# A transformer-style block in fp32 products on one core: two of the four weight sums move to GpSimd, and spills and reloads to SyncE's queue

## The chip, the core and the metric

The kernel runs on one core of a Trainium2 chip. The metric is device time in microseconds (us); lower is better. Engines are named as the profile does: PE (TensorE; PEld is its weight load), DVE (VectorE), ACT (ScalarE), POOL (GpSimd), SP (SyncE, which here issues DMAs only).

## What is computed

One layer of a streaming encoder with 256 rows, 2048 columns, in fp32. Cut to its products:

```python
h = rms_norm(x, norm_mix)
proj = h @ w_in                       # 2048 x 11264: two mixers and two gates
y_a = hgrn2_mixer(...)                # gated recurrence
y_b = chunked_relpos_attention(...)
merged = sigmoid(gate_a) * (y_a @ w_proj_a) + sigmoid(gate_b) * (y_b @ w_proj_b)
x = x + merged @ w_out                # 2048 x 2048
h = rms_norm(x, norm_ffn)
g, u = split(h @ w_ffn_in)            # 2048 x 11264
x = x + (silu(g) * u) @ w_ffn_out     # 5632 x 2048
```

## The kernel before

**Products.** Every weight is read once, in blocks of 512 rows by 512 columns; a block arrives as two tiles `raw` of 128x1024 (512 KB each; eight buffers). An fp32 product is made of three products of rounded parts: ACT casts a weight tile to `whi`, DVE subtracts to get the rest, `wlo`, and PE runs three matmuls (high by high, high by low, low by high) for each tile of activations and columns. `whi` and `wlo` have four buffers each. In a plain product (`product`, lines 156 to 173) each `raw` costs one cast (L147) and one subtraction (L148).

**Pairs of products.** `product_pair` (L206 and on) works on two column blocks at once and saves one eighth of PE's work in chosen steps: in one use of 512 rows, the first two of four k-tiles go through seven products instead of eight (a Strassen scheme in Winograd's form), the other two go plainly. The seven products need sums of weights. `weight_forms` (L185 to L203) makes them on DVE from four quarter tiles b11, b21, b12, b22 of 128x512: `ta` = (b12 - b11, b22 - b12) and then `tb` = (ta0 - b22, b21 + tb0), all four through the helper at L194; each pair is split into `whi` and `wlo` as a raw tile is (`halves`, `split`, L177 and L178). `ta` and `tb` share two buffers (tag `t6`), so the next `ta` waits until the last one is split. There are 46 uses: gate blocks (2 pairs of products, 4 uses each), w_out (1 pair, 4 uses), w_ffn_in (5 pairs, 4 uses each) and w_ffn_out (2 pairs, 7 uses each of 11 steps). A pair with four uses is called a stage below.

**Order of work.** A scheduler in the language's tile layer sets each engine's order from priorities; `high_priority` in `product_pair` lets the weight preparation run ahead of the matmuls it is for, as far as buffers allow. Each engine then works through its own list in order, and waits on semaphores.

**Sums of activations.** `act_forms` (L318) makes the activation side of the seven products (`sf`, then a split into `fm`, `fx`, `fq`, `sform`); its inputs in `transpose_split` (L305) come from PE transposes in PSUM. In the first feed-forward product the sums of seven steps (`sform`) are spilled to DRAM (`kept`, L315) and read back before the last product (`sf`, L907). The residual `x` is spilled at L843 and read back at L912; `x_forms` (L753) reads quarter rows of `x_t` again at L759. In the kernel before, these five kinds of DMA are issued by POOL; all weights are issued by SP (L130), in a list of its own that also waits in order.

The lines that the change touches are L194 to L198 in `weight_forms`, and L315, L759, L843, L907 and L912.

Of the kernel before, what the change touches and what calls it, by code (L numbers as in the profile page):

```python
# [10 lines left out]
F32 = mybir.dt.float32  # L11
# [3 lines left out]
ALU = mybir.AluOpType  # L15
# [30 lines left out]
def block_kernel(ctx: ExitStack, tc: tile.TileContext, x, x_t, w_in, w_pa, w_pb, w_out, w_fi, w_fo,  # L46
                 params, b_gate, bias, masks, out):
    nc = tc.nc
# [14 lines left out]
    def nm(s):  # L63
        uid[0] += 1
        return f"{s}_{uid[0]}"

    def t4(shape, s, dt=F32):
        return big.tile(shape, dt, tag="t4", name=nm(s))
# [29 lines left out]
    def add(out, a, b):  # L98
        nc.vector.tensor_tensor(out=out, in0=a, in1=b, op=ALU.add)
# [18 lines left out]
    def start(g):  # L118
        running.append(g)
# [60 lines left out]
    def halves(src):  # L180

        n = src.shape[1]
        hi = whi_p.tile([P, 2, 512], F32R, tag="hi", name=nm("whi"))
        lo = wlo_p.tile([P, 2, 512], F32R, tag="lo", name=nm("wlo"))
        split(hi[:, 0:n, :], lo[:, 0:n, :], src)  # L185
        return [(hi[:, k, :], lo[:, k, :]) for k in range(n)]

    def weight_forms(r0, r1):


        ta = t6_p.tile([P, 2, 512], F32, tag="t6", name=nm("ta"))
        tb = t6_p.tile([P, 2, 512], F32, tag="t6", name=nm("tb"))
        b11, b21, b12, b22 = r0[:, 0, :], r0[:, 1, :], r1[:, 0, :], r1[:, 1, :]
        op = lambda out, x, y, o: nc.vector.tensor_tensor(out=out, in0=x, in1=y, op=o)  # L194
        p1, p2 = halves(r0)
        p3, = halves(r1[:, 1:2, :])
        op(ta[:, 0, :], b12, b11, ALU.subtract)
        op(ta[:, 1, :], b22, b12, ALU.subtract)  # L198
        p5, p7 = halves(ta)
        op(tb[:, 0, :], ta[:, 0, :], b22, ALU.subtract)  # L200
        op(tb[:, 1, :], b21, tb[:, 0, :], ALU.add)
        p6, p4 = halves(tb)
        return {1: p1, 2: p2, 3: p3, 4: p4, 5: p5, 6: p6, 7: p7}  # L203
# [72 lines left out]
    def split_tiles(s):  # L276
        return (t4([P, 4, T], s + "h", F32R), t4([P, 4, T], s + "l", F32R))
# [11 lines left out]
    def transpose_split_pair(nat, pair, hi, lo, gain=None, pool=aux):  # L289

        pt = transpose_pair(nat, pair, pool)
        if gain is None:
            sl = slice(2 * pair, 2 * pair + 2)
            nc.scalar.copy(hi[:, sl, :], pt)
            nc.vector.tensor_tensor(out=lo[:, sl, :], in0=pt, in1=hi[:, sl, :].bitcast(F32),
                                    op=ALU.subtract)
            return pt
        for j in range(2):
            k = 2 * pair + j
            nc.scalar.activation(hi[:, k, :], pt[:, j, :], AF.Copy, scale=gain[:, k:k + 1])  # L300
            nc.vector.scalar_tensor_tensor(out=lo[:, k, :], in0=pt[:, j, :],
                                           scalar=gain[:, k:k + 1],
                                           in1=hi[:, k, :].bitcast(F32),
                                           op0=ALU.mult, op1=ALU.subtract)
        return pt  # L305

    def transpose_split(nat, hi, lo, gain=None, wait=2, pool=aux, forms=None, spill=None):
        for _ in range(wait):
            yield 1
        for pair in range(2):  # L310
            pt = transpose_split_pair(nat, pair, hi, lo, gain, pool)
            if forms is not None and pair == 0:
                act_forms(pt, forms, gain)
                if spill is not None:
                    nc.gpsimd.dma_start(out=spill, in_=forms.bitcast(F32))  # L315
            yield 1

    def act_forms(pt, f, gain=None):  # L318

        s = t2([P, 4, P], "sf")  # L320
        a11, a21, a12, a22 = (pt[:, k, m * P:(m + 1) * P] for k in range(2) for m in range(2))

        def op(out, x, k, y, o):
            if gain is None:
                nc.vector.tensor_tensor(out=out, in0=x, in1=y, op=o)
            else:
                nc.vector.scalar_tensor_tensor(out=out, in0=x, scalar=gain[:, k:k + 1], in1=y,
                                               op0=ALU.mult, op1=o)

        if gain is None:  # L330
            nc.scalar.copy(s[:, 2, :], a21)
        else:
            nc.scalar.activation(s[:, 2, :], a21, AF.Copy, scale=gain[:, 0:1])
        op(s[:, 0, :], a22, 1, s[:, 2, :], ALU.add)
        op(s[:, 2, :], a11, 0, s[:, 2, :], ALU.subtract)
        op(s[:, 1, :], a11, 0, s[:, 0, :], ALU.subtract)
        op(s[:, 3, :], a12, 1, s[:, 1, :], ALU.add)
        split(f[:, 0], f[:, 1], s)
# [9 lines left out]
    xs = []  # L348
# [4 lines left out]
    def sumsq_block(src, ss, c):  # L353
        for m in range(2):
            junk = t2([P, 512], "junk")
            nc.scalar.activation(junk, src[:, m, :], AF.Square, accum_out=ss[:, m, c:c + 1])
# [228 lines left out]
    def hgrn_mix(half, b, kk, qT, v, sg, hi, lo):  # L585
# [26 lines left out]
        for i in range(2):  # L612
# [15 lines left out]
            for h in range(4):  # L628
# [3 lines left out]
                                               op0=ALU.mult, op1=ALU.mult)  # L632
            yield 1
        yield from transpose_split(y, hi, lo, gain, wait=2)


# [118 lines left out]
    def x_forms():  # L755

        for c in range(4):
            xt = t4([P, 2, T], "xt2")
            nc.gpsimd.dma_start(out=xt, in_=x_t[c, :, 0:2, :])  # L759
            fq[c] = t4([P, 2, 4, P], "fq", F32R)  # L760
            yield 1
            yield 1
            act_forms(xt, fq[c], par[:, C_NM + 4 * c:C_NM + 4 * c + 4])

    gates, fq = {}, {}
    start(x_forms())
    for nb in range(4):
        bgs, gts = [], []
        for br in range(2):
            c = 4 * br + nb  # L770
# [6 lines left out]
            for m in range(2):  # L777
                nc.vector.scalar_tensor_tensor(out=gt[:, m, :], in0=ps[m], scalar=r1[:, m:m + 1],
                                               in1=bgs[br], op0=ALU.mult, op1=ALU.add)
# [37 lines left out]
    x2T, x2_kept, fx = [], [], {}  # L817
    ss2 = cpool.tile([P, 2, 4], F32, tag="ss2", name="ss2")
    r2 = cpool.tile([P, 2], F32, tag="r2", name="r2")
    def residual_sums(x0, x1):  # L820
        def sums(ub):
            u2, u3 = t2([P, 512], "u2"), t2([P, 512], "u3")
            add(x0[:, 0, :], x0[:, 0, :], ub[1])
            nc.scalar.copy(u2, ub[1])
            add(u2, ub[6], u2)
            add(u3, ub[7], u2)
            add(x1[:, 0, :], x1[:, 0, :], u2)
            add(x0[:, 1, :], x0[:, 1, :], u3)
            add(x1[:, 1, :], x1[:, 1, :], u3)
            for m in range(2):  # L830
                add(x1[:, m, :], ub[5], x1[:, m, :])
        return sums

    def norm_block(nb, ps):
        for m in range(2):
            add(xs[nb][:, m, :], ps[m], xs[nb][:, m, :])
        x2T.append(split_tiles("x2T"))
        fx[nb] = t4([P, 2, 4, P], "fx", F32R)
        start(transpose_split(xs[nb], *x2T[nb], gain=par[:, C_NF + 4 * nb:C_NF + 4 * nb + 4],
                              forms=fx[nb]))  # L840
        sumsq_block(xs[nb], ss2, nb)
        x2_kept.append(dram.tile([P, 2, 512], F32, tag=f"x2_{nb}", name=nm("x2")))
        nc.gpsimd.dma_start(out=x2_kept[nb], in_=xs[nb])  # L843

    for pair in range(2):
        nbs = (2 * pair, 2 * pair + 1)
# [13 lines left out]
    kept = {}  # L860
# [22 lines left out]
    for j in range(NJ):  # L883
# [12 lines left out]
        if j in SEVEN:  # L896
            f = t4([P, 2, 4, P], "sform", F32R)
            spill = kept[j] = dram.tile([P, 2, 4, P], F32, tag=f"kept{j}", name=nm("kept"))
# [5 lines left out]
    forms = {}  # L904
    for j in SEVEN:
        forms[j] = t4([P, 2, 4, P], "sf", F32R)
        nc.gpsimd.dma_start(out=forms[j].bitcast(F32), in_=kept[j])  # L907
    for pair in range(2):
        nbs = (2 * pair, 2 * pair + 1)
        xs = {nb: t4([P, 2, 512], "x2") for nb in nbs}  # L910
        for nb in nbs:
            nc.gpsimd.dma_start(out=xs[nb], in_=x2_kept[nb])  # L912
        x0, x1 = (xs[nb] for nb in nbs)

        pools = (mm, aux) if pair == 0 else (aux, mm)
        cb = product_pair(w_fo, nbs, NJ, act_h, forms, *pools,
                          residual_sums(x0, x1), last=pair == 1)
        for n, nb in enumerate(nbs):
            for m in range(2):
                pieces = 2 if nb == 3 and m == 1 else 1  # L920
                w = 512 // pieces
                for i in range(pieces):
                    sl = slice(i * w, (i + 1) * w)
                    add(xs[nb][:, m, sl], cb[m, n][:, sl], xs[nb][:, m, sl])
                    nc.sync.dma_start(out=out_v[:, m, nb * 512 + i * w:nb * 512 + (i + 1) * w],
                                      in_=xs[nb][:, m, sl])
# [63 lines left out]
```

## Time and profile before

| what | value |
|---|---|
| median of 3 runs | 1428.09 us (1427.48 to 1429.13) |
| the profiled execution, its own time | 1427.22 us |
| its span in the profile | 1425.4 us |
| PE busy | 1417.6 us (99%) |
| DVE busy | 1063.6 us (75%) |
| ACT busy | 774.2 us (54%) |
| POOL busy | 50.1 us (4%) |
| DMA, mean | 202 GB/s |

The span is what the trace covers; the time of the run is 1.8 us longer. Busy shares are averages over the whole span. Whether an engine is on the path is read from what the next engine was waiting for at that moment, and with how much to spare.

### The profile page before, as it was taken

Reading aid. Unit: us, or ns where it says so; the run is one execution under the profiler, and the core shown is the slowest. Engines: PE = TensorE matmul, PEld = TensorE weight load, DVE = VectorE, ACT = ScalarE, POOL = GpSimd, SP = SyncE. Lnnn points to the kernel's source line nnn. Section 1 sums busy time; section 2 is a strip of 40 time slices with the busy share of each in tenths; the row PEclk is TensorE's granted clock in tenths of the full one; section 3 lists DMA queues with packets and bytes.
Section 4 is the critical chain, followed back from the end, with each engine's and each line's share of the span. In section 5 each row is a group of like instructions: output and inputs, shape, how many; then the busy total and the mean of one; then the engine's idle time right before and its main releaser. Section 6 shows DMA issues by size and latency. Waiting matters only on the chain.

```text
span 1425.4 us, 17596 instructions
## 1 busy us (share of the span) xinstructions
PE 1417.6 (99%) x6448; PEld 1174.4 (82%) x6448; DVE 1063.6 (75%) x1361; ACT 774.2 (54%) x1009; POOL 50.1 (4%) x63
## 2 busy tenths in 40 slices
PE   9999999999999999999999999999999999999998
PEld 7888888888888888878888888888788888888887
DVE  6768869564878697689767769687796876777875
ACT  7756565555655454455555546455454554544553
POOL 0100100100000000100000000000000010000000
PEclk9999999999999999999999999999999999999999
DMA  9654354446657556547654657656476578666652
GB/s 360 243 192 161 134 193 156 164 163 195 222 183 240 197 197 210 184 148 239 220 203 168 228 169 240 206 179 228 164 238 206 178 254 303 210 221 221 208 183 84
DMA packets 81848, 288.37 MB, mean 202 GB/s; under 512 B 9185, under 2 KB 9441, under 8 KB 81761
## 3 DMA queue, kind: packets, MB, share of 16 engines
q1 hardware_dynamic: 78272, 274.66, 57.5%
q0 software_dynamic: 3488, 12.58, 2.3%
q8 instruction: 50, 0.82, 0.2%
q14 instruction: 38, 0.30, 0.1%
HBM read 279.34 MB, written 7.86 MB: 201 GB/s over the span
## 4 chain that ended last, share of the span: by engine, by line
PE 98%; DVE 1%; ACT 0%; DMA 0%; issue 0%; SPq 0%; DVEq 0%; ACTq 0%
PE mm L169 18%; PE mm L168 18%; PE mm L170 18%; PE mp L223 13%; PE mp L224 13%; PE mp L222 13%; PE bank L285 2%; PE bank L543 1%; DVE wlo L178 1%; ACT whi L177 0%; PE bank L573 0%; DMA raw<-in_w_in 0%; PE bank L619 0%; PE bank L670 0%; PE bank L698 0%; DVE tb L194 0%
## 5 line engine op out<-in xcount | busy, mean ns | idle before, releaser
L148 DVE TENSOR_TENSOR wlo<-raw,whi 128x1024 fp32r<-128x1024 f32 (+1 forms) x292 | 351.9, 1212 | 175.6 <-ACT whi L147 173.4
L147 ACT CAST whi<-raw 128x1024 fp32r<-128x1024 f32 (+1 forms) x292 | 301.9, 1040 | 292.7 <-PE mm L170 219.8
L178 DVE TENSOR_TENSOR wlo<-raw,whi 128x1024 fp32r<-128x1024 f32 x216 | 235.0, 1110 | 51.9 <-ACT whi L177 50.8
L177 ACT CAST whi<-raw 128x1024 fp32r<-128x1024 f32 x216 | 201.2, 960 | 121.8 <-PE mp L224 59.6
L168 PE MATMUL mm<-whi,xTh 128*128 128x512 f32 x576 | 226.6, 398 | 1.3 <-ACT whi L147 1.3
L169 PE MATMUL mm<-wlo,xTh 128*128 128x512 f32 x576 | 225.2, 391 | 0.0
L170 PE MATMUL mm<-whi,xTl 128*128 128x512 f32 x576 | 225.1, 391 | 0.0
L168 PE MATMUL mm<-whi,x2Th 128*128 128x512 f32 x384 | 150.0, 391 | 0.0
L170 PE MATMUL mm<-whi,x2Tl 128*128 128x512 f32 x384 | 149.5, 389 | 0.0
L169 PE MATMUL mm<-wlo,x2Th 128*128 128x512 f32 x384 | 149.4, 389 | 0.0
L168 PEld LDWEIGHTS mm<-whi,xTh 128*128 128x128 f32 x576 | 108.2, 188 | 23.0 <-ACT whi L147 2.0
L170 PEld LDWEIGHTS mm<-whi,xTl 128*128 128x128 f32 x576 | 108.2, 188 | 22.6
L169 PEld LDWEIGHTS mm<-wlo,xTh 128*128 128x128 f32 x576 | 108.3, 188 | 21.8 <-DVE wlo L148 1.0
L223 PE MATMUL mp<-wlo,hTh 128*128 128x512 f32 x282 | 109.7, 389 | 0.0
L224 PE MATMUL mp<-whi,hTl 128*128 128x512 f32 x282 | 109.6, 389 | 0.0
L222 PE MATMUL mp<-whi,hTh 128*128 128x512 f32 x282 | 99.7, 390 | 0.0
L177 ACT CAST whi<-ta 128x1024 fp32r<-128x1024 f32 x46 | 48.3, 1050 | 89.9 <-PE mp L224 87.4
L178 DVE TENSOR_TENSOR wlo<-ta,whi 128x1024 fp32r<-128x1024 f32 x46 | 56.2, 1223 | 48.3 <-ACT whi L177 48.3
L224 PE MATMUL mp<-whi,x2Tl 128*128 128x512 f32 x220 | 86.2, 392 | 0.0
L223 PE MATMUL mp<-wlo,x2Th 128*128 128x512 f32 x220 | 86.2, 392 | 0.0
L170 PEld LDWEIGHTS mm<-whi,x2Tl 128*128 128x128 f32 x384 | 72.1, 188 | 15.0
L168 PEld LDWEIGHTS mm<-whi,x2Th 128*128 128x128 f32 x384 | 72.1, 188 | 14.8
(256 smaller groups left out, 2260.8 us busy)
## 6 DMA issues: line engine op xcount, KB each, us to landing
raw<-in_w_fi SPq DMA_DIRECT2D x176, 512.0 KB, 4.4
raw<-in_w_in SPq DMA_DIRECT2D x172, 512.0 KB, 4.1
raw<-in_w_fo SPq DMA_DIRECT2D x88, 512.0 KB, 5.3
raw<-in_w_out SPq DMA_DIRECT2D x32, 512.0 KB, 4.3
raw<-in_w_pa SPq DMA_DIRECT2D x16, 512.0 KB, 3.7
raw<-in_w_pb SPq DMA_DIRECT2D x16, 512.0 KB, 4.3
x<-x POOLq DMA_DIRECT2D x8, 512.0 KB, 5.7
kept<-sform POOLq DMA_DIRECT2D x7, 512.0 KB, 4.9
```

The costliest lines, as they stand in the source:

```text
L147: nc.scalar.copy(hi[:, sl, :], src[:, sl, :])
L148: nc.vector.tensor_tensor(out=lo[:, sl, :], in0=src[:, sl, :], in1=hi[:, sl, :].bitcast(F32), op=ALU.subtract)
L168: nc.tensor.matmul(ps[m], lhsT=ah, rhs=wh, start=kc == 0 and k4 == 0, stop=False)
L169: nc.tensor.matmul(ps[m], lhsT=ah, rhs=wl, start=False, stop=False)
L170: nc.tensor.matmul(ps[m], lhsT=al, rhs=wh, start=False, stop=kc == n_chunks - 1 and k4 == 3)
L177: nc.scalar.copy(hi, src)
L178: nc.vector.tensor_tensor(out=lo, in0=src, in1=hi.bitcast(F32), op=ALU.subtract)
L222: nc.tensor.matmul(ps, lhsT=ah, rhs=wh, start=first, stop=False)
L223: nc.tensor.matmul(ps, lhsT=ah, rhs=wl, start=False, stop=False)
L224: nc.tensor.matmul(ps, lhsT=al, rhs=wh, start=False, stop=final)
L285: nc.tensor.transpose(out=pt[:, j, m * P:(m + 1) * P], in_=nat[:, m, c:c + P], identity=ident)
L543: nc.tensor.matmul(pl[:, j, :], lhsT=ek[:, g // 2, (g % 2) * P:(g % 2 + 1) * P], rhs=eq[:, g, :], start=True, stop=True)
```

## The change

Two of the four sums in `weight_forms` (those of `ta`) are issued on GpSimd instead of VectorE, 92 instructions in all. The 26 DMAs that POOL issued (four reads of `x_t`, four spills of `x`, seven spills of `sform`, their seven and four reloads) are issued by SyncE's queue.

```diff
@@ weight_forms
-        op(ta[:, 0, :], b12, b11, ALU.subtract)
-        op(ta[:, 1, :], b22, b12, ALU.subtract)
+        for i, (x, y) in enumerate(((b12, b11), (b22, b12))):
+            nc.gpsimd.tensor_tensor(out=ta[:, i, :], in0=x, in1=y, op=ALU.subtract)
         p5, p7 = halves(ta)
@@ transpose_split
-                    nc.gpsimd.dma_start(out=spill, in_=forms.bitcast(F32))
+                    nc.sync.dma_start(out=spill, in_=forms.bitcast(F32))
@@ x_forms
-            nc.gpsimd.dma_start(out=xt, in_=x_t[c, :, 0:2, :])
+            nc.sync.dma_start(out=xt, in_=x_t[c, :, 0:2, :])
@@ norm_block
-        nc.gpsimd.dma_start(out=x2_kept[nb], in_=xs[nb])
+        nc.sync.dma_start(out=x2_kept[nb], in_=xs[nb])
@@ before the last product
-        nc.gpsimd.dma_start(out=forms[j].bitcast(F32), in_=kept[j])
+        nc.sync.dma_start(out=forms[j].bitcast(F32), in_=kept[j])
...
-            nc.gpsimd.dma_start(out=xs[nb], in_=x2_kept[nb])
+            nc.sync.dma_start(out=xs[nb], in_=x2_kept[nb])
```

The scheduler puts the new lists together. On DVE, in the w_ffn_in stage around 943 us of the profile (the numbers behind names tell buffers apart: ta_7922 is the `ta` of this use, tb_7840 the `tb` of the use before, raw_7833 and raw_7837 weight tiles that go plainly):

```order
 L178 TENSOR_TENSOR wlo_7852<-ta_7839,whi_7851 128x1024
 L178 TENSOR_TENSOR wlo_7858<-tb_7840,whi_7857 128x1024
-L194 TENSOR_TENSOR ta_7922<-raw_7918,raw_7914 128x512
-L194 TENSOR_TENSOR ta_7922<-raw_7918 128x512
 L178 TENSOR_TENSOR wlo_7862<-raw_7833,whi_7861 128x1024
+L194 TENSOR_TENSOR tb_7923<-ta_7922,raw_7918 128x512
 L178 TENSOR_TENSOR wlo_7866<-raw_7837,whi_7865 128x1024
-L194 TENSOR_TENSOR tb_7923<-ta_7922,raw_7918 128x512
 L178 TENSOR_TENSOR wlo_7925<-raw_7914,whi_7924 128x1024
```

The two subtractions leave DVE's list, and the first sum of `tb` moves up by one instruction, ahead of the split of raw_7837.

On SP's list, where the last product begins, around 1197 us of the profile (raw tiles are weights of w_ffn_out, the x tiles the residual's third and fourth block, read back):

```order
 L130 DMA raw_10102<-in_w_fo 128x1024
 L130 DMA raw_10104<-in_w_fo 128x1024
+L912 DMA x_2185_10752<-x_1153_5807 128x1024
+L912 DMA x_2186_10753<-x_1188_5990 128x1024
 L130 DMA raw_10106<-in_w_fo 128x1024
 L130 DMA raw_10108<-in_w_fo 128x1024
```

The two reloads now stand between weight loads, and raw_10106 is issued behind whatever they wait for.

## Rows read from the trace of the kernel before

**Rows 1.** The page, part 1: busy time of each engine, share, instructions.

```profile
PE 1417.6 (99%) x6448; PEld 1174.4 (82%) x6448; DVE 1063.6 (75%) x1361; ACT 774.2 (54%) x1009; POOL 50.1 (4%) x63
```

**Rows 2.** Waits: who waited for whom, us in total, times, longest.

```profile
PEld mp L222 <- ACT whi L177: 3.2, 6, 1.0
PEld mp L223 <- DVE wlo L178: 2.5, 7, 0.5
```

**Rows 3.** Groups by line: busy us, mean ns of one.

```profile
L194 DVE TENSOR_TENSOR ta<-raw,raw 128x512 f32<-128x512 f32 x46 | 32.1, 697 | 15.8 <-DMA raw<-in_w_fi 8.2 <-DMA raw<-in_w_fo 4.3 <-DMA raw<-in_w_in 1.8
L194 DVE TENSOR_TENSOR ta<-raw 128x512 f32<-128x512 f32 x46 | 31.5, 685 | 0.0
```

**Rows 4.** DVE's busy time in one stage of w_ffn_in (stretch, length, busy).

```profile
930.00:971.00 41.00, 35.75 (x42) 1.00 0.55 185
```

**Rows 5.** Line 809 on POOL: duration ns min/median/max.

```profile
L809 POOL TENSOR_TENSOR gate<-gate,gate x8: 1293/1521/2280, 554.9 to 624.5; 128x512 f32<-128x512 f32 x8
```

**Rows 6.** Timeline of POOL, 62 to 65 us: start, us, engine, line, operation.

```profile
62.33 2.01 POOL L559 COPY eq<-qT 128x1024 f32<-128x1024 f32 x1 [23.88 <-DVE qT L473]
64.28 1.07 POOL L521 COPY eq<-b 128x512 f32<-128x512 f32 x1
```

**Rows 7.** Timeline of DVE, the same stretch.

```profile
62.21 1.23 DVE L148 TENSOR_TENSOR wlo<-raw,whi 128x1024 fp32r<-128x1024 f32 x1
63.35 1.52 DVE L564 TENSOR_TENSOR eq<-eq,qT 128x512 f32<-128x512 f32 x1
```

**Rows 8.** Timeline of DVE, 934 to 949 us, a stage of w_ffn_in.

```profile
934.53 1.23 DVE L178 TENSOR_TENSOR wlo<-ta,whi 128x1024 fp32r<-128x1024 f32 x1 [2.29 <-ACT whi L177]
...
937.96 1.23 DVE L178 TENSOR_TENSOR wlo<-tb,whi 128x1024 fp32r<-128x1024 f32 x1 [0.26 <-ACT whi L177]
...
942.64 1.22 DVE L178 TENSOR_TENSOR wlo<-ta,whi 128x1024 fp32r<-128x1024 f32 x1
943.92 1.23 DVE L178 TENSOR_TENSOR wlo<-tb,whi 128x1024 fp32r<-128x1024 f32 x1
945.06 0.69 DVE L194 TENSOR_TENSOR ta<-raw,raw 128x512 f32<-128x512 f32 x1
...
946.26 2.36 DVE L178 TENSOR_TENSOR wlo<-raw,whi 128x1024 fp32r<-128x1024 f32 x2
948.54 0.69 DVE L194 TENSOR_TENSOR tb<-ta,raw 128x512 f32<-128x512 f32 x1
```

**Rows 9.** Timeline of PE: first matmuls on the two tiles of the x2 row above.

```profile
947.56 0.48 PE L223 MATMUL mp<-wlo,x2Th 128*128 128x512 f32 x1
...
950.17 0.39 PE L223 MATMUL mp<-wlo,x2Th 128*128 128x512 f32 x1
```

**Rows 10.** Timeline of DVE, 857 to 862 us, a stage with activation sums in it.

```profile
857.17 1.22 DVE L178 TENSOR_TENSOR wlo<-tb,whi 128x1024 fp32r<-128x1024 f32 x1
...
859.51 1.22 DVE L178 TENSOR_TENSOR wlo<-raw,whi 128x1024 fp32r<-128x1024 f32 x1
...
861.85 2.96 DVE L178 TENSOR_TENSOR wlo<-raw,whi 128x1024 fp32r<-128x1024 f32 x3
```

**Rows 11.** Timeline of PE: first matmul on the first tile of the x3 row above.

```profile
863.88 0.39 PE L223 MATMUL mp<-wlo,x2Th 128*128 128x512 f32 x1
```

**Rows 12.** Timeline of DVE in the last product, at a use behind a use.

```profile
1211.51 1.22 DVE L178 TENSOR_TENSOR wlo<-ta,whi 128x1024 fp32r<-128x1024 f32 x1 [1.40 <-ACT whi L177]
...
1214.23 1.23 DVE L178 TENSOR_TENSOR wlo<-tb,whi 128x1024 fp32r<-128x1024 f32 x1 [0.17 <-ACT whi L177]
```

**Rows 13.** Timeline of PE: first matmul on the last tile of rows 12.

```profile
1216.57 0.39 PE L223 MATMUL mp<-wlo,sf 128*128 128x512 f32 x1
```

**Rows 14.** Timeline of POOL: a spill, and the last reload.

```profile
861.74 0.53 POOL L315 DMA_DIRECT2D kept<-sform  x1 [44.39 <-DVE sform L178]
...
1202.80 0.54 POOL L912 DMA_DIRECT2D x<-x  x1 [11.05 <-PE bank L285]
```

**Rows 15.** Timeline of SP: the weight loads that stand around these two.

```profile
860.75 2.67 SPq L130 DMA_DIRECT2D raw<-in_w_fi  x2
...
1206.66 0.33 SPq L130 DMA_DIRECT2D raw<-in_w_fo  x1
```

## The prediction

> **What bounds the kernel now.** I read the shares first: PE is busy in 99% of the span, DVE in 75%, POOL in 4% [rows 1]. The reader is to see from this that relief on DVE can buy little by itself: PE never lacks work for long. The waits come next: in the pairs of products, PE's weight loads waited for a cast 6 times, 3.2 us in all, and for DVE's `wlo` 7 times, 2.5 us [rows 2]. These 5.7 us are about all that a faster preparation of weights could give back there. The third view is a stage by itself: in a stage of w_ffn_in DVE is busy 35.75 of 41 us [rows 4], far more than its average. The fourth is the timeline inside such a stage, with DVE's and PE's rows side by side. There DVE works without a gap from 942.64 to 949 us [rows 8], and its two splits of plain weights end at about 947.5 and at 948.62 (946.26 + 2.36). PE takes the first up at 947.56 and the second at 950.17 [rows 9]; which matmul uses which tile I took from the numbers in the two lists. So the spare time is nearly nothing for the one and 1.55 us for the other. The stage runs at PE's speed, but with DVE close behind: whatever delays DVE there by more than a microsecond reaches PE.
>
> **The change, part by part.**
>
> *What leaves DVE.* 92 subtractions of 0.69 us, 63.6 us busy [rows 3]. They follow each other closer than that: two take the time from 945.06 to 946.26, so 0.60 us each [rows 8], and 1.2 us for each of 46 uses.
>
> *What POOL takes on.* POOL already does the same operation on the same shape at L809: 1293 ns at best, 2280 ns at worst [rows 5]. I take 1.29 us as the run by itself. 92 of them are 119 us on an engine that is busy for 50 us [rows 1], so POOL as such does not become a bound.
>
> *What the two engines do to each other.* This is the term that decides. At 62.21 DVE starts a split with two operands in SBUF; its next instruction is issued at 63.35 and shows 1.52 us for 512 columns, where 0.69 is usual [rows 3, 7]. POOL's copy is issued at 62.33 and shows 2.01 us; the next, at 64.28, shows 1.07 us for half the columns [rows 6]. Laid side by side: POOL waits until the split ends at 63.4 and runs to 64.3; DVE's next, issued in between, waits until 64.3 and runs to 64.9; only then POOL's next one runs. They take turns, whole instructions at a time, and the one that has waited goes first. The spread at L809 fits, since 2.28 is 1.29 and most of a split of 1.22. So while both have work, each POOL subtraction stops DVE for 1.29 us and saves it 0.60. A use costs DVE between -1.2 us (POOL hits idle time, or a DVE instruction that reads one operand from PSUM) and 2 x (1.29 - 0.60) = +1.4 us. In gapless stretches I take the upper value, in others I follow the rows.
>
> [...]
>
> *An ordinary stage, worked through.* The next `ta` may start once the last one is split (two shared buffers). First use: the split of `ta` ends at 935.76 (934.53 + 1.23). POOL runs to 937.1 and to 938.4. DVE's split of `tb` could start at 937.96 [rows 8], so it is 0.44 late, and the chain behind it is packed. Next use: the split of `ta` ends at 943.86, DVE's split of `tb` starts at 943.92 and is ahead of POOL. It hands over after 1.14 us (945.06). Then in turn: POOL to 946.35, DVE's first plain split to 947.49, POOL to 948.78, DVE's sum `tb` to 949.38 (it now stands ahead of the second plain split), and the second plain split ends 1.22 later, at 950.60. Before it ended at 948.62. PE wants it at 950.17: 0.43 late. With the 0.44 carried in, PE loses 0.9 us in this stage. Three stages of w_ffn_in (930 us is the middle one) and two of the gates have this shape: 5 x 0.9 = 4.4 us.
>
> *The stages with activation sums.* Where the step before has its sums spilled, `act_forms` falls into the stage and DVE has no gap at all. After the split of `tb` at 857.17 POOL takes over at 858.31 (to 859.60), DVE's plain split, before at 859.51, hands over at 860.74, POOL runs to 862.03. Then `tb` and the split of `sform`, 0.60 each, to 863.23, and the next plain split ends at 864.45. Before it ended at 863.07 (861.85 + 1.22) [rows 10]; PE wants it at 863.88 [rows 11]: 0.57 late, with the same 0.44 carried in 1.0. There are three such stages (w_out, and two of w_ffn_in): 3.0 us.
>
> *The last product.* Its margins are wider. The split of `ta` ends at 1212.73, POOL runs to 1214.1 and 1215.4, so the split of `tb` starts 1.15 late, not at 1214.23, and ends at 1216.6 [rows 12]; PE wants it at 1216.57 [rows 13]. That is some 0.1 us where a use follows a use directly, 8 times: 0.8 us. The six others lie beside steps without sums, and I cost them at nothing; that work hides up to 2.6 us each.
>
> *The DMAs.* 26 issues go from POOL's list to SP's. SP waits in order, so a reload that waits for a buffer would hold up weights. But the scheduler put each behind a weight load that was issued late enough already: the spill that POOL issued at 861.74 comes between two loads issued from 860.75 on and ending at 863.42, and the last reload, which waited until 1202.80, stands ahead of a load that was issued only at 1206.66 [rows 14, 15]. I cost them at 0. If that cover went, a load would be later by the difference, and DVE's and ACT's lists would wait for the weights behind it. The four reads of `x_t` come later than before, on the way to sums that are needed only in the first gate stage: 0.
>
> *Sum.* 4.4 + 3.0 + 0.8 + 0 = +8.2 us, on the profiled execution's own 1427.22 us: **1435.4 us**. That execution lies 0.9 us under the median of the runs. Neither end of the unknown is far: without any collision the gain is at most the 5.7 us of rows 2; with every margin used up by the full 1.4 us in all 46 uses the loss would be 64 us, but DVE has 5.25 us to spare in a stage of 41 [rows 4], against 4 x 1.4 = 5.6. So a stage can hardly lose more than 2 us, 16 in all.
>
> **The rivals.** About 0.2% (2.9 us) is what a measurement of this kernel can tell from no change.
>
> 1. *The collisions stay hidden.* If POOL's pairs mostly fall into DVE's idle time, or a first delay of PE buys spare time for all that follows, the losses stay under 2.9 us: 1427 to 1430. For it speaks that PE's lateness is not added up use by use, against it the 0.1 us to spare at 947.56. Chance 0.20.
>
> 2. *DVE's relief reaches PE: faster.* The waits of rows 2 sit in the stages with activation sums, where DVE has no gap; there it sheds 1.2 us in each use. If POOL needs little of the shared way, these 5.7 us shrink by more than half, and the time is 1423 to 1424. The point that decides: POOL's subtraction must delay DVE by less than the 0.60 that it saves. Rows 6 and 7 show 0.8 beside a copy. [...]
>
> 3. *DVE always goes first.* If POOL got its turn only in DVE's gaps, `ta` would come late by several us, the cast of `ta` would hold up ACT's list, and each of some 30 uses in stages would cost 2 us: 1487. Rows 6 and 7 show that the waiting engine goes first. Chance 0.02, in the tail.
>
> 4. *SP's list blocks.* One reload that waits for its buffer in front of weights, as rows 14 show one waiting 11 us, would cost up to that much once the eight `raw` buffers are used up: 1439 or more, if some order of waits isn't as I read it. Chance 0.05, counted with the slower cases.
>
> That the sums do not move at all is excluded by POOL's list, where all 92 stand.
>
> **How the numbers follow.** The forecast has 0.65 and, with rivals 3 and 4, slower has 0.72; rival 1 is the same, 0.20; rival 2 is faster, 0.08. The range of 8 in 10 takes in rival 1 and the stage losses up to 2 us each: 1427.5 to 1444. The forecast's own range is 1431 to 1443.
>
> **What would show it.** In the profile after: POOL's subtractions at 1.3 us at best and near 2.4 where DVE is busy; the splits of `tb` and of plain weights stretched to about 2.4 us in the stages; DVE's busy time not lower by 64 us but about the same or higher; waits of PE's weight loads for `wlo` of some 8 us more, in the eight stages; the reloads on SP without waits that move weights. Wrong would be: splits that keep 1.22 us beside POOL's work, PE's waits unchanged, or a loss that sits at the start of the last product instead.

## The result and the profile after

The changed kernel takes 1441.68 us (median of 4 runs, 1441.38 to 1442.17), the kernel before beside it 1428.61 us (4 runs, 1427.48 to 1430.26): 1.0088 times as long, 95% interval 1.0074 to 1.0102, or 13.1 us slower. 1435.4 us was predicted: the sign is right and the result inside the range, but the size is a good third too small. The profiled execution after took 1441.79 us, its span 1440.0.

The page's part 1 of the kernel after, which answers to [rows 1]:

```profile
PE 1424.5 (99%) x6448; PEld 1173.4 (81%) x6448; DVE 1064.4 (74%) x1269; ACT 773.6 (54%) x1009; POOL 180.0 (13%) x129
```

DVE runs 92 instructions fewer and is just as long busy as before. Its groups by line and form, and POOL's (busy us, mean ns of one | idle before), answer to [rows 3]:

```profile
L178 DVE TENSOR_TENSOR wlo<-raw,whi 128x1024 fp32r<-128x1024 f32 x170 | 219.3, 1312 | 40.9 <-ACT whi L177 40.8
...
L178 DVE TENSOR_TENSOR wlo<-tb,whi 128x1024 fp32r<-128x1024 f32 x46 | 76.1, 1654 | 36.0 <-ACT whi L177 35.7
L198 POOL TENSOR_TENSOR ta<-raw 128x512 f32<-128x512 f32 x46 | 74.3, 1616 | 0.0
L198 POOL TENSOR_TENSOR ta<-raw,raw 128x512 f32<-128x512 f32 x46 | 71.8, 1560 | 716.8 <-DVE wlo L178 355.4 <-DMA raw<-in_w_fi 197.4 <-DMA raw<-in_w_fo 102.1
...
L194 DVE TENSOR_TENSOR tb<-ta,raw 128x512 f32<-128x512 f32 x46 | 53.0, 1152 | 20.1 <-POOL ta L198 20.0
```

The time that the two sums gave up came back in the instructions that stand beside POOL's: the split of `tb` shows 1654 ns in the mean where one split by itself shows 1.22 us [rows 8], the first sum of `tb` 1152 ns where a sum by itself shows 0.69 us. The waits after, which answer to [rows 2]:

```profile
DVE tb L194 <- POOL ta L198: 20.0, 14, 2.1
PEld mp L223 <- DVE wlo L178: 16.9, 36, 1.3
...
PE mp L223 <- DVE wlo L178: 5.3, 14, 0.8
PEld mp L222 <- ACT whi L177: 5.0, 8, 1.1
```

PE's weight loads waited for `wlo` 7 times before and 36 times now, for 14.4 us more (16.9 - 2.5; some 8 were forecast). The first line looks like a price too: DVE stands 20 us waiting for `ta`. It costs next to nothing: 7 of the 14 waits lie at the first uses of stages and 5 in the last product, and a run of experiment 4 that keeps 11 of them (17.1 us) loses 0.4 us in its stages and its last product together.

**Where the time went.** Both programs run the same 6448 matmuls, in the same order but for 150 places in short groups (the fills kernel of experiment 2 has 165 such places, at no loss), so the start of the k-th in one trace can be set against the k-th in the other. How far the changed kernel has fallen behind:

| part | predicted, us | fell behind, us |
|---|---|---|
| first 20 us | 0 | 2.2 |
| two gate stages | 0.9 each | 1.75 and 1.70 |
| w_out | 1.0 | 1.4 |
| w_ffn_in, three ordinary stages | 0.9 each | 1.26 each |
| w_ffn_in, two with activation sums | 1.0 each | 1.5 each |
| last product | 0.8 | 0.4 |

Between the stages nothing is lost. The stages make 11.7 us, the last product 0.4, together 12.1 against 8.2. With the 2.2 us of the start and 0.3 us behind the last matmul they are the 14.6 us between the two profiled executions (1441.79 - 1427.22).

**Inside a stage.** The w_ffn_in stage of [rows 4] and [rows 8] now lies some 10 us later. Timeline of DVE after, last two uses:

```profile
954.04 1.23 DVE L178 TENSOR_TENSOR wlo<-tb,whi 128x1024 fp32r<-128x1024 f32 x1
955.18 2.33 DVE L178 TENSOR_TENSOR wlo<-raw,whi 128x1024 fp32r<-128x1024 f32 x1
957.44 1.78 DVE L194 TENSOR_TENSOR tb<-ta,raw 128x512 f32<-128x512 f32 x1
959.13 2.35 DVE L178 TENSOR_TENSOR wlo<-raw,whi 128x1024 fp32r<-128x1024 f32 x2
...
964.12 2.15 DVE L178 TENSOR_TENSOR wlo<-tb,whi 128x1024 fp32r<-128x1024 f32 x1 [0.30 <-ACT whi L177]
966.20 2.31 DVE L178 TENSOR_TENSOR wlo<-raw,whi 128x1024 fp32r<-128x1024 f32 x1
968.44 0.68 DVE L194 TENSOR_TENSOR tb<-ta,raw 128x512 f32<-128x512 f32 x1
```

Timeline of POOL, the same stretch:

```profile
954.06 2.37 POOL L198 TENSOR_TENSOR ta<-raw,raw 128x512 f32<-128x512 f32 x1 [5.83 <-DVE wlo L178]
956.40 2.27 POOL L198 TENSOR_TENSOR ta<-raw 128x512 f32<-128x512 f32 x1
963.90 1.30 POOL L198 TENSOR_TENSOR ta<-raw,raw 128x512 f32<-128x512 f32 x1 [5.24 <-DVE wlo L178]
965.16 2.28 POOL L198 TENSOR_TENSOR ta<-raw 128x512 f32<-128x512 f32 x1
```

The turns are as forecast. At 954.04 DVE's split is 0.02 ahead: POOL waits for it (2.37), DVE's next waits for POOL (2.33), POOL's second for that (2.27), and `tb` for POOL (1.78). At 963.90 POOL comes first, alone (1.30), and the split of `tb` beside it takes 2.15. Then they alternate again. The split that starts at 966.20 ends at 968.51, and PE, whose last matmul on ready weights is the third of the x3 row, takes it up at once (timeline of PE):

```profile
967.36 0.84 PE L222 MATMUL mp<-whi,x2Th 128*128 128x512 f32 x3
968.57 0.50 PE L223 MATMUL mp<-wlo,x2Th 128*128 128x512 f32 x1 [0.37 <-DVE wlo L178]
```

In the kernel before the same place reads so, DVE first, then PE:

```profile
953.95 1.22 DVE L178 TENSOR_TENSOR wlo<-tb,whi 128x1024 fp32r<-128x1024 f32 x1
955.08 1.22 DVE L178 TENSOR_TENSOR wlo<-raw,whi 128x1024 fp32r<-128x1024 f32 x1
```

```profile
956.98 0.84 PE L222 MATMUL mp<-whi,x2Th 128*128 128x512 f32 x3
957.65 0.39 PE L223 MATMUL mp<-wlo,x2Th 128*128 128x512 f32 x1
```

There the split ended at 956.30, 1.35 us ahead of PE's 957.65. PE moved 10.38 us up to this place (967.36 - 956.98), the split's end 12.21 (968.51 - 956.30): 1.83 us later against PE, more than the spare 1.35. The stall and what it leaves behind cost 0.66 us. The sums that do it are those of the stage's fourth use; they run beside the splits of its third, as each use's sums run beside the splits of the one before. The prediction worked this out for the sums of the second and third use and left the fourth out.

### The profile page after: what moved, and what is told of

Its sections match the earlier page's. It is cut to its first block, busy times and chain, and to the rows that moved or that the text cites. A ratio compares the mean times of both kernels' runs of the same rounds, so it can differ in the third digit from the quotient of the medians.

```text
span 1440.0 us, 17725 instructions
## 1 busy us (share of the span) xinstructions
PE 1424.5 (99%) x6448; PEld 1173.4 (81%) x6448; DVE 1064.4 (74%) x1269; ACT 773.6 (54%) x1009; POOL 180.0 (13%) x129
## 4 chain that ended last, share of the span: by engine, by line
PE 92%; DVE 5%; ACT 1%; issue 1%; POOL 0%; DMA 0%; SPq 0%; DVEq 0%; ACTq 0%
PE mm L168 18%; PE mm L169 18%; PE mm L170 18%; PE mp L223 11%; PE mp L224 11%; PE mp L222 11%; DVE wlo L178 4%; PE bank L285 2%; PE bank L543 1%; ACT whi L177 1%; POOL ta L198 0%; DMA raw<-in_w_in 0%; DVE tb L194 0%; PE bank L573 0%; PE bank L619 0%
## 5 line engine op out<-in xcount | busy, mean ns | idle before, releaser
L178 DVE TENSOR_TENSOR wlo<-raw,whi 128x1024 fp32r<-128x1024 f32 x216 | 250.6, 1181 | 46.7 <-ACT whi L177 46.7
L198 POOL TENSOR_TENSOR ta<-raw,raw 128x512 f32<-128x512 f32 x46 | 71.8, 1560 | 716.8 <-DVE wlo L178 355.4
L178 DVE TENSOR_TENSOR wlo<-tb,whi 128x1024 fp32r<-128x1024 f32 x46 | 76.1, 1654 | 36.0 <-ACT whi L177 35.7
L177 ACT CAST whi<-tb 128x1024 fp32r<-128x1024 f32 x46 | 48.3, 1050 | 67.3 <-PE mp L224 56.6
```

Source lines behind the costliest of these rows:

```text
L177: nc.scalar.copy(hi, src)
L178: nc.vector.tensor_tensor(out=lo, in0=src, in1=hi.bitcast(F32), op=ALU.subtract)
L198: nc.gpsimd.tensor_tensor(out=ta[:, i, :], in0=x, in1=y, op=ALU.subtract)
```

## The experiments

How far each kernel's matmuls fall behind those of the profiled execution before, as above (the last column is the median time):

| kernel | first 20 us | stages | last product | us |
|---|---|---|---|---|
| the change | 2.2 | 11.7 | 0.4 | 1441.68 |
| sums alone | 1.2 | 11.7 | 0.4 | 1440.73 |
| transfers alone | 2.7 | 0.0 | 0.0 | 1428.96 |
| one sum of two | 1.1 | 6.7 | 0.0 | 1434.75 |
| fills in place of sums | 1.6 | -0.7 | 0.0 | 1428.02 |
| last use on VectorE | -0.2 | 7.1 | 0.4 | 1434.84 |
| only first use on GpSimd | 2.2 | 0.0 | 0.4 | 1429.20 |
| four sums | 0.7 | 17.3 | 0.2 | 1445.49 |
| two more, nobody waits | 1.8 | 23.7 | 1.8 | 1455.18 |

**1. The two halves of the change.** Sums alone: the five DMA lines back to `nc.gpsimd`. Transfers alone:

```diff
-        for i, (x, y) in enumerate(((b12, b11), (b22, b12))):
-            nc.gpsimd.tensor_tensor(out=ta[:, i, :], in0=x, in1=y, op=ALU.subtract)
+        op(ta[:, 0, :], b12, b11, ALU.subtract)
+        op(ta[:, 1, :], b22, b12, ALU.subtract)
```

> The two ta subtractions of each use on GpSimd as in the change; the spills and reloads stay on GpSimd's queue. Theory (VectorE and GpSimd take turns on SBUF, so VectorE's sums and low parts come late): the five ordinary stages and the three with activation sums keep the whole loss, about 12.0 us by the drift of the products between the two traces, so 1440.6 us; 1441 to 1442 if the 2.6 us that are lost in the first 18 us come with the sums too. Rival (the loss is that of the transfers, late or in the way on SyncE's queue): 1428.6 us, as before.

> The spills and reloads issued from SyncE's queue as in the change; all four weight sums stay on VectorE. Theory: no stage loses anything, 1428.6 us; if the 2.6 us of the first 18 us follow GpSimd's empty queue, 1431.2 us. Rival (the loss is that of the transfers): about 1440 us.

Sums alone: 1440.73 us, ratio 1.0088 (1.0075 to 1.0102). Transfers alone: 1428.96, ratio 1.0002 (0.9994 to 1.0011). The whole loss is that of the sums; the transfers are worth nothing either way, as costed. The first column settles the 2.2 us of the start (2.6 us in the expectations, which is too much): it follows no part of the change. It is largest (2.7 us) in a kernel whose time is that of before, and eight of the nine kernels lie behind the one profiled execution of before, which at 1427.22 us is among its fastest. What differs can be read in the stretch from 10 to 15 us (length, busy us of PE, PEld, DVE, ACT and POOL, granted clock, DMA share, GB/s), before, then after, then with the transfers alone:

```profile
10.00:15.00 5.00, 5.00 (x23) 3.94 (x22) 4.54 (x9) 4.24 (x10) 0.00 (x0) 1.00 1.03 399
```

```profile
10.00:15.00 5.00, 5.00 (x19) 4.02 (x18) 4.50 (x9) 4.28 (x10) 0.00 (x0) 0.80 1.04 413
```

```profile
10.00:15.00 5.00, 5.00 (x16) 3.95 (x15) 4.53 (x9) 4.43 (x10) 0.00 (x0) 1.00 1.05 411
```

PE is busy for all of the 5.00 us each time, yet gets 23, 19 and 16 matmuls into them. Before, the matmuls start some 0.23 us apart from 8.17 us on. After the change they start 0.43 us apart until 12.05 us, with the transfers alone until 13.40 us, and 0.23 us apart from there on. That is about half the pace. The granted clock of the row is lower after the change (0.80), but not with the transfers alone (1.00), so no run shows what sets the pace. Ahead of this PE had waited 1.28, 2.61 and 1.87 us for the cast of the first weights; why that wait differs from one execution to another stays open. One execution's first 20 us differ by up to 2.8 us from another's, and a comparison of two traces has to take that off first.

**2. No reads.** GpSimd writes a constant of the same size into `ta`, six fills in place of two subtractions; the sums of `ta` are not computed. The engines behind wait for `ta` as in the change. The fills themselves do not wait for weights, which the subtractions did in 13 of the 46 uses:

```diff
-        for i, (x, y) in enumerate(((b12, b11), (b22, b12))):
-            nc.gpsimd.tensor_tensor(out=ta[:, i, :], in0=x, in1=y, op=ALU.subtract)
+        for i in (0, 0, 0, 1, 1, 1):
+            nc.gpsimd.memset(ta[:, i, :], 1.0)
```

> The change with GpSimd filling ta with a constant, three times over each half so that GpSimd is as long at it, where the subtractions stood: ta is not computed, all waits on it stay. Theory (the price is that two-input subtractions of both engines hold each other up at SBUF): a fill reads nothing, VectorE's instructions keep their alone times (0.60 and 1.10 to 1.2 us), and the loss of the stages is gone: 1428 to 1431 us, 2.6 us more at most if the start is lost here too. Rival (the price is ta arriving late from another engine): the same waits of VectorE for ta, 1438 us or more.

1428.02 us, ratio 0.9995 (0.9986 to 1.0004): nothing is left of the loss. Its page's part 1, groups and waits:

```profile
PE 1417.5 (99%) x6448; PEld 1175.9 (82%) x6448; DVE 1009.4 (71%) x1269; ACT 773.7 (54%) x1009; POOL 168.0 (12%) x313
```

```profile
L198 POOL MEMSET ta<- 128x512 f32 x276 | 132.0, 528 | 728.0 <-DVE wlo L178 725.0 <-PE bank L543 2.9
...
L178 DVE TENSOR_TENSOR wlo<-tb,whi 128x1024 fp32r<-128x1024 f32 x46 | 56.3, 1225 | 45.8 <-ACT whi L177 45.5
```

```profile
PEld mp L223 <- DVE wlo L178: 1.8, 4, 0.6
```

`ta` is ready 2.87 us after its start here (six fills of 0.53 us), later than a pair of subtractions alone (2.55 us), and nobody suffers. So the hand-over as such is not the price. In the change a pair beside a busy DVE takes up to 4.8 us, and no fill copies that; that so late a `ta` is not the price either is shown only by experiment 5, where nobody waits for GpSimd. What is left is GpSimd's reading of SBUF, which the fills leave out. The two kernels run the same 1269 DVE instructions, in 1009.4 and 1064.4 us: 55.0 us over 92 subtractions, so a stop of 0.60 us each in the mean, about half of the 1.1 us by which one that falls on a busy DVE stops it (2.33 us against 1.22). Three things are seen here. A split, which has two operands in SBUF, shows 2.33 us beside a subtraction and 1.22 by itself. The fills, which only write to SBUF, were not in the way: 528 ns each, the splits beside them 1225 ns. And the one that came second waited for nearly the whole of the other: the subtraction that came 0.02 us behind a split shows 2.37 us, where by itself it takes 1.29.

The run also tells what there was to win. With the sums off DVE at no price, and a `ta` that takes 2.87 us, the stages gain 0.7 us: so little is the relief of DVE worth.

**3. One sum of two.**

```diff
-        for i, (x, y) in enumerate(((b12, b11), (b22, b12))):
-            nc.gpsimd.tensor_tensor(out=ta[:, i, :], in0=x, in1=y, op=ALU.subtract)
+        op(ta[:, 0, :], b12, b11, ALU.subtract)
+        nc.gpsimd.tensor_tensor(out=ta[:, 1, :], in0=b22, in1=b12, op=ALU.subtract)
```

> The change with only the second of the two ta subtractions (b22 minus b12) on GpSimd, the first back on VectorE. Theory of taking turns: one GpSimd subtraction costs VectorE about 1.29 us and takes 0.60 us off it, so VectorE comes 0.69 us later per use instead of 1.38 us; the margin of 0.9 to 1.5 us that it has on TensorE in an ordinary use covers most of that, and under a third of the 12.0 us of the stages stays: 1429 to 1433 us, up to 2.6 us more if the start is lost here too. Rival (the price is that of the hand-over between the engines, VectorE waiting for a ta made elsewhere): the wait for the second ta is still there in each use, and at least half of the loss stays: 1435 us or more.

1434.75 us, ratio 1.0046 (1.0033 to 1.0058): between the two theories, and a miss. The five ordinary stages lose 0.50 to 0.55 us each and w_out 0.7. The two with activation sums lose 1.7 us each, more than with both sums moved. There the turns fail. Timeline of POOL, DVE and ACT in the first of them (other instructions left out; DVE has no idle time between 860.31 and 868.14):

```profile
860.31 0.28 DVE L325 TENSOR_TENSOR sf<-bank,sf 128x128 f32<-128x128 f32 x1
...
860.48 8.82 POOL L198 TENSOR_TENSOR ta<-raw 128x512 f32<-128x512 f32 x1 [6.86 <-DVE wlo L178]
860.51 1.22 DVE L178 TENSOR_TENSOR wlo<-tb,whi 128x1024 fp32r<-128x1024 f32 x1
...
861.65 0.68 DVE L194 TENSOR_TENSOR ta<-raw,raw 128x512 f32<-128x512 f32 x1
...
862.25 1.22 DVE L178 TENSOR_TENSOR wlo<-raw,whi 128x1024 fp32r<-128x1024 f32 x1
...
867.46 0.68 DVE L194 TENSOR_TENSOR tb<-raw,tb 128x512 f32<-128x512 f32 x1
...
869.33 1.05 ACT L177 CAST whi<-ta 128x1024 fp32r<-128x1024 f32 x1 [4.70 <-POOL ta L198]
```

POOL's subtraction gets no turn while DVE works through nine instructions at their own pace. It ends 1.16 us after DVE's last (868.14 to 869.30), and the cast of `ta`, with ACT's list behind it, waits 4.70 us. The same stands once in the other such stage, again 8.82 us. In the change itself the trace has two of 3.55 us at the same places, with two splits let by, and so have the traces of the sums alone and of experiment 4's first kernel.

**4. Which use.** In the eight stages the last chunk's sums back on VectorE, and then only the first chunk's on GpSimd (`kc != 3` becomes `kc == 0`):

```diff
-    def weight_forms(r0, r1):
+    def weight_forms(r0, r1, gps):
...
-            nc.gpsimd.tensor_tensor(out=ta[:, i, :], in0=x, in1=y, op=ALU.subtract)
+            (nc.gpsimd if gps else nc.vector).tensor_tensor(out=ta[:, i, :], in0=x, in1=y, op=ALU.subtract)
...
-                        tf = weight_forms(r[0][0], r[1][0])
+                        tf = weight_forms(r[0][0], r[1][0], kc != 3 or n_chunks > 4)
```

> The change, but in the eight four-chunk stages the two ta subtractions of the last chunk (kc = 3) are back on VectorE; the other three uses of each stage and the last product keep theirs on GpSimd. Theory (each use has its own collision, and the prediction left out the one of the last use): the 0.66 us by which the products fall behind at the last use of each of the eight stages go, 5.3 us of the 13.1, so 1436.4 us (1435.5 to 1437.5). Rival (the stall at the last use is the lateness of the earlier uses that comes due there): it stays, 1440 us or more.

> The change, but in the eight four-chunk stages only the first chunk (kc = 0) has its two ta subtractions on GpSimd, the other three on VectorE; the last product keeps its 14 uses on GpSimd. Theory: at the first use of a stage the products do not fall behind in the changed kernel, and the last product loses 0.4 us, so 1428.6 to 1429.6 us, no difference from before. Rival 1 (the first use's lateness is carried into the second): 8 x 0.2 to 0.4 us more, 1430.5 to 1432 us. Rival 2 (at last VectorE is relieved and nothing collides in a margin that matters): under 1428 us.

Without the last use: 1434.84 us, ratio 1.0046 (1.0034 to 1.0059), under the expected 1435.5 to 1437.5. In the matmuls 4.6 us of the 11.7 are gone: 0.6 to 0.7 in each of seven stages, nothing in w_out, where I had counted it too. The profiled execution is 7.4 us under the change's, and the other 2.8 are no part of the stages: its start came 2.37 us sooner (first column) and what follows the last matmul was 0.46 us shorter. Only the first use: 1429.20, ratio 1.0003 (0.9995 to 1.0012), the stages at 0.0 and the last product at 0.4, as expected. The loss is made use by use, by the sums of the second, third and fourth, and none by those of the first.

**5. More of it.** All four sums on GpSimd (`tb` through `nc.gpsimd.tensor_tensor` as well), and, apart from that, two subtractions more that nobody waits for:

```diff
         op(ta[:, 0, :], b12, b11, ALU.subtract)
         op(ta[:, 1, :], b22, b12, ALU.subtract)
+        nc.gpsimd.tensor_tensor(out=scratch, in0=b12, in1=b11, op=ALU.subtract)
+        nc.gpsimd.tensor_tensor(out=scratch, in0=b22, in1=b12, op=ALU.subtract)
```

> The change with all four sums of each use (ta and tb) on GpSimd. Theory: VectorE's sums of 0.60 us go, four stops of 1.29 us come, 2.8 us later per use instead of 1.4, beyond the margins in every use of a stage, and tb, made by two subtractions that depend on each other, comes late besides: the loss more than doubles, 26 us or more, so 1455 us or more, most likely 1465 to 1490 us. Rival (with nothing but splits left VectorE has so much idle time that GpSimd's turns fall into it): no more loss than the change, 1442 us or less.

> The kernel before, all four sums of each use on VectorE and the transfers on GpSimd's queue, with two subtractions of the same operands more on GpSimd in each use, into a scratch tile that nobody reads: no engine waits for a sum made elsewhere. Theory (each GpSimd subtraction stops VectorE for 1.29 us): VectorE is busy 35.75 of 41 us in a stage before; eight stops make 10.3 us more, so it would need 46 us, and it comes 2.6 us later per use instead of 1.4 as in the change: the stages lose more than twice as much, 25 to 50 us, 1454 to 1480 us. If only those stops count that do not fall into VectorE's idle time, as the four-sums run suggests, not less than the change's loss: 1441 us. Rival (the price of the change is the wait for ta): 1428.6 us, as before.

In the second kernel the transfers stood on SyncE's queue, not on GpSimd's as the text has it; by experiment 1 that is worth nothing. It takes 1455.18 us, ratio 1.0187 (1.0170 to 1.0204), as the theory has it. No engine and no weight load waits for GpSimd's result, and the loss is twice that of the change (27.3 us against 13.1). DVE's busy time, in its page's part 1, grew by 74.2 us over the same 1361 instructions [rows 1], 0.81 us for each of 92:

```profile
PE 1427.3 (98%) x6448; PEld 1173.3 (81%) x6448; DVE 1137.8 (78%) x1361; ACT 773.7 (53%) x1009; POOL 194.5 (13%) x129
```

Four sums on GpSimd miss the expectation of 1455 us or more by 9.5 us: 1445.49, ratio 1.0118 (1.0103 to 1.0134). I had counted four full stops of 1.29 us. DVE's busy time is 1084.2 us; the fills kernel's 1009.4 less its sums of `tb` (31.9 and 31.5) would be 946.0, so 184 stops took 0.75 us each, and DVE shed 2.4 us a use. A stop is to be priced by its chance of meeting a busy DVE, not at its worst.

**6. The turns by themselves.** Small kernels with nothing in them but a list of DVE instructions and one GpSimd subtraction (in one case three) beside it, in 75 cases with both operands in SBUF (13, 20, 20 and 22) and two others:

```python
def dve(n, in0=None, w=1024):
    for k in range(n):
        nc.vector.tensor_tensor(out=los[k][:, 0:w], in0=g[:, 0:w],
                                in1=b[:, 0:w] if in0 is None else in0, op=sub)
```

> The collision by itself: none of the block is computed and the output is a constant. VectorE runs eight subtractions (128x1024, two operands in SBUF) from one list without a wait between them, GpSimd one 128x512 subtraction beside them; GpSimd's is released by the same ScalarE copy as VectorE's first, or after a fill of growing length, or VectorE's are put off by a short copy, or GpSimd's waits for VectorE's first. Then VectorE reads one operand from PSUM, then it runs instructions with one operand, and at the end each engine is alone. Theory of the prediction (whole instructions in turn, the one that has waited goes first): wherever GpSimd's comes, it waits for at most one VectorE instruction and shows 1.3 to 2.5 us, and one VectorE instruction shows 1.2 more. Rival (seen in the half-moved kernel, where one GpSimd subtraction shows 8.82 us): when it comes at the same moment as VectorE's first, or a few hundredths of a microsecond before, it waits until VectorE's list runs empty, 8 x 1.14 + 1.3 = 10.4 us, and VectorE keeps its 1.22 us. Beside PSUM operands GpSimd should show 1.29 us by both.

> The collision by itself once more; none of the block is computed and the output is a constant. Twenty cases copy what stood before the two 8.82 us subtractions of the half-moved kernel: VectorE runs a short subtraction with one operand in PSUM (16 to 192 columns), then eight subtractions with two operands in SBUF without a wait between them; GpSimd's one subtraction is released beside the short one, in ten cases by the same ScalarE copy, in ten by the end of a VectorE split ahead of it. If the order of arrival decides (GpSimd issued while VectorE is at an instruction with a PSUM operand, its next one 0.04 us later), some of the cases show about 10 us and VectorE at 1.22 us, in a band of widths; otherwise all show 1.3 to 2.5 us, and what held GpSimd off in the kernel stays open.

> The collision by itself, a third time; none of the block is computed and the output is a constant. Twenty cases rebuild the wait that stood before the 8.82 us subtractions: VectorE makes a sum, then a split whose end releases GpSimd's subtraction, then (in twelve cases) a 128-column subtraction from PSUM, then eight splits, the first of which waits for a ScalarE cast of the sum; the cast's length (832 to 1120 columns) moves the release of that split past the moment at which GpSimd's subtraction comes. If a VectorE instruction that is let go by a semaphore within some hundredths of a microsecond of GpSimd's can hold GpSimd off for the whole list behind it, one or two of the cases show 9 us or more with VectorE at 1.22 us; if not, all show 1.3 to 2.5 us, and what held GpSimd off in the kernel stays open.

> As the run before (nothing of the block is computed, the output is a constant), with the cast long enough that it is what releases VectorE's first split: 22 cases, 1120 to 1456 columns in steps of 16, so that the split's start moves from ahead of GpSimd's subtraction to some 0.25 us behind it in steps of about 0.015 us; the kernel's case, 0.04 us behind, lies inside. If that release holds GpSimd off for the whole list, a case or two show 9 us or more; if not, GpSimd's subtraction shows about 2.3 us up to the crossing and about 1.3 us behind it, and the cause stays open.

The last three ask what held GpSimd off in experiment 3. In the third the cast was too short to release the split, so its cases all came with VectorE ahead; the fourth mends that. Timeline of the last of them, two neighbouring cases of the sweep, in which DVE's list (the x3 and x2 rows hold its first instructions) starts together with POOL's subtraction and 0.02 us behind it:

```profile
121.69 2.35 POOL L76 TENSOR_TENSOR pa<-first,b 128x512 f32<-128x512 f32 x1 [12.81 <-ACT h L70]
121.69 4.56 DVE L75 TENSOR_TENSOR lo<-b,h 128x1024 fp32r<-128x1024 f32 x3
...
136.84 1.26 POOL L76 TENSOR_TENSOR pa<-first,b 128x512 f32<-128x512 f32 x1 [12.81 <-ACT h L70]
136.86 3.46 DVE L75 TENSOR_TENSOR lo<-b,h 128x1024 fp32r<-128x1024 f32 x2
```

At the tie DVE goes first (POOL shows 2.35 us); when DVE comes 0.02 us behind, POOL does (1.26 us). Wherever DVE's instructions have two operands in SBUF, the theory of turns holds: POOL waits for at most one (1.26 to 2.35 us in the first and the last of the four), then DVE's next shows 2.2 to 2.3 us, and three GpSimd subtractions in a row (6.58 us) alternate with three of DVE's. Timeline of the first of the four, where DVE reads one operand from PSUM, and where it has one operand only:

```profile
193.20 4.28 DVE L68 TENSOR_TENSOR lo<-g,ps 128x512 f32<-128x512 f32 x7 [2.94 <-ACT g L64]
193.31 1.27 POOL L76 TENSOR_TENSOR pa<-g,b 128x512 f32<-128x512 f32 x1 [8.67 <-ACT g L64]
...
200.96 4.17 DVE L73 TENSOR_SCALAR lo<-g 128x1024 f32<-128x1024 f32 x5 [2.89 <-ACT g L64]
201.07 1.70 POOL L76 TENSOR_TENSOR pa<-g,b 128x512 f32<-128x512 f32 x1 [6.50 <-ACT g L64]
```

Beside DVE's instructions with a PSUM operand POOL shows the 1.27 us that it takes by itself, and seven of DVE's take 4.28. Beside one-operand instructions from SBUF to SBUF POOL is held up as well (1.70). None of the 75 cases shows the 8.82 us, the last sweep included, in which the first split's start passes POOL's in steps of some 0.015 us. What kept GpSimd from its turn in the kernel stays open.

No version came out faster than the kernel before, and the fills kernel says why none was to be looked for in this direction: 0.7 us in the stages is all that it gained.

## Why the prediction was right, and where it was not

*The turns, and the sign.* Right. One GpSimd subtraction takes 1.3 us alone and up to 2.4 beside a busy DVE (but for the two of 3.55), the splits beside it up to 2.35, DVE's busy time is 1064.4 against 1063.6 us, and PE's waits for `wlo` grew. A stop is 1.1 us in the timelines (2.33 - 1.22), not the 1.29 that was reckoned. That the reading is the cause was argued from [rows 6, 7]; experiments 2 and 5 show it.

*"Three stages of w_ffn_in and two of the gates have this shape: 5 x 0.9."* The step that failed. It works out the collisions of two uses' sums and stops there. Those of the fourth use meet a spare time of 1.35 us with a delay of 1.83: 0.6 to 0.7 us in seven of the eight stages, 4.6 us. That is more than the whole difference between 12.1 and 8.2, because the two collisions that were worked through cost 0.22 and 0.38 in the ordinary stages of w_ffn_in, where 0.44 and 0.43 were reckoned. In the gate stages they cost 1.05, of which 0.48 arises where PE waits for the cast of a late `tb`.

*"Three stages with activation sums, 3.0 us."* 1.5 each in w_ffn_in, of which 0.8 to 0.9 lies in the collisions that were worked out, against 1.0; the fourth use's sums are again what was missing. In w_out it is 1.4 without them.

*The last product, 0.8 us.* 0.4: the 0.1 us was right, the count was not. In the trace PE falls behind by 0.1 us at four places of the last product, not at eight. The 5 of DVE's 14 waits for `ta` that lie there (9.3 us) fall at other places and cost nothing.

*The DMAs, 0.* Right, by experiment 1.

*The rivals.* The collisions did not stay hidden, and DVE's relief reached PE by 0.7 us at best. "DVE always goes first" got a 0.02 and is wrong as a rule, but it exists: the two stages in which it happened make half of what one moved sum costs. SP's list blocked nothing.

*The base.* The error of 6.3 us (1441.68 - 1435.4) is 3.9 from the stages and the last product (12.1 - 8.2), 1.4 from the base, since the sum stood on one short execution (1428.61 - 1427.22), and 1.0 that is left within what executions differ by.

## What to carry to other kernels

Moving elementwise work to GpSimd did not relieve VectorE here: it was busy for 1064.4 us after and 1063.6 before. Beside VectorE's instructions with two operands in SBUF each GpSimd subtraction, which reads two as well, stopped VectorE by up to 1.1 us and by 0.60 to 0.81 us in the mean of three kernels, and it takes nearly twice as long as the one it replaces (1.29 us against 0.69). Beside a PSUM operand, in a small kernel, it took its 1.27 us, and in the first uses of the stages the sums cost nothing (0.0 us). Before pricing such a move, find out with the cheapest stand-in, a fill of the same length, what the relief is worth at best; here 0.7 us of 1428. Such a fill shows nothing of what the reads cost; two reads that nobody waits for (experiment 5) do. And walk every use of a stage against the consumer's clock: the one left out held over a third of the loss.

## What the runs showed of the hardware that was not expected

- In the last sweep the order at the crossing is sharp: VectorE first at a tie (GpSimd's subtraction 2.35 us), GpSimd first when it leads by 0.02 us (1.26).
- Two subtractions of 8.82 us in one kernel and two of 3.55 us in three others, at the same places of the program, behind nine and two VectorE instructions that ran on at their own pace; 75 cases made for it did not bring it back.
- A VectorE instruction with one operand from SBUF holds GpSimd up too (1.70 us instead of 1.26, in one case), and GpSimd's fills, which read nothing, held nothing up and were not held up (516 to 537 ns each, the splits at their 1.22 us).
- The first 20 us of an execution vary by up to 2.8 us without any change that bears on them: PE's matmuls stay at 0.43 us apart, half their later pace, until 12.05 us in one and 13.40 in another, and in the one of before they start 0.23 us apart from 8.17 us on.
